# The input norm's weight row multiplied into x instead of into the weights, and head norms by Exp(-0.5 Ln a) with one Newton step

## The chip, the cores and the metric

The kernel runs on one core of a Trainium2 chip. A core has a matrix engine (TensorE, PE in the profile; its weight loads are listed apart as PEld) and three engines for everything else: VectorE (DVE), ScalarE (ACT) and GpSimd (POOL). Each takes its instructions in order from a queue of its own, and semaphores hold an instruction back until what it needs is there. SyncE (SP) issues the transfers between the core's memory (SBUF) and the chip's memory, in order too. TensorE writes to accumulator banks (PSUM). The metric is the device time of one execution in microseconds.

## The reference

One encoder block on x of 2048 rows by 1024, in float32. What matters here:

```python
def rms_norm(x, gain):
    y = x * lax.rsqrt(jnp.mean(x * x, axis=-1, keepdims=True) + EPS)
    return y * gain

h = rms_norm(x, norm_gain)          # norm_gain: one weight for each of the 1024 columns
proj = h @ w_in                     # q, k, v of mixers A and B, gates ga and gb, merge gates mg
qa = rms_norm(qa.reshape(bsz, S, 8, 64), q_norm_a) * scale     # head norms: 64 columns each
ka = rms_norm(ka.reshape(bsz, S, 2, 64), k_norm_a)             # and the same for qb, kb
ya = banded_attention(qa, ka, va, ...) * silu(ga)
yb = merged(dilated_group(qb[g], kb[g], vb[g], ...) for g in 3 groups) * silu(gb)
merged = sigmoid(mg0 + b0) * (ya @ w_branch_a) + sigmoid(mg1 + b1) * (yb @ w_branch_b)
out = x + merged @ w_out
```

The weight row of the first norm may be multiplied into the normed rows or into the rows of w_in: the product is the same. A head norm needs 1/sqrt(a) of one number a for each row and head.

## The kernel before

Every large product is made of float16 matmuls: each operand is split into a high part and a remainder ("hi" and "lo"; XH and XL of x, wh and wl of the weights), and three products are added. Each block of weights is first scaled by a power of two, found from its sum of squares. The program has three stages.

*The x stage (0 to 71 us).* Sixteen tiles of 128 rows of x are loaded. ScalarE squares each and sums along the row (`x_square`, L432). `x_stats` makes a of the sums of a group of tiles, and `x_newton` 1/sqrt(a); there are five groups, two of two tiles and three of four. VectorE multiplies the tile (`x_scale`, L446), TensorE transposes it in two halves into one of three PSUM buffers (L452), ScalarE copies a half out as XH (L455), VectorE writes XL (L459). When four tiles are done, TensorE starts on two columns of gates (`g_step`, matmuls of 128 by 512, L294), with further transposes in between. The gate weights graw are multiplied by the norm's weights on GpSimd (`g_gain`, L309), squared, scaled and split.

*The unit stage (71 to about 1305 us).* 14 units of eight pairs of row blocks each, 112 pairs: two units of kind A (16 pairs) and twelve of kind B, three for each of four head pairs. For a pair TensorE makes q, k and v (L620) into two PSUM banks (pj) that take turns. ScalarE copies q and k out (rw, L638) and the high part of v (vt, L650), VectorE the remainder of v (L656), which frees the bank. Then the head norm: ScalarE squares (L663), VectorE sums (L668, L669), a first guess of 1/sqrt(a) from the bits of a (`rs_guess`, L245), three Newton steps on GpSimd (`rs_newton`, L254 to L257), the product with it on VectorE (L680), the product with the head weights on GpSimd (L687), the split on ScalarE (L693), VectorE (L697) and GpSimd (L702), and a transposing transfer to kq. Attention follows some three pairs later: scores (L770), maxima (L785), exponentials (L793), a high part (p, L798) and a remainder (L802), a transposing transfer to pt, values (L819). In the third unit of each head pair (32 pairs in all, "merge pairs" below) the three groups of mixer B are also merged: small operations on VectorE (L964 to L977), products on GpSimd (L982), sums on VectorE (L988, L989).

Beside this, one unit ahead, the next unit's weights are loaded to wraw, multiplied by the norm's weights on GpSimd (`w_gain`, in four parts, L165), squared on ScalarE (L203), summed by a small matmul (L179) and split (L220, L226).

*The tail (from about 1305 us).* Merge gates, two more gates, the branch products and the output product, with sums of blocks that save one product in eight. Sums of blocks of x and their splits (L1171 to L1180) are VectorE's work. Here the weights' gain is on ScalarE (`gain` in `w_ready`, L1229), before the squares (L1235); L1304 and L1305 finish a gate.

The order on every engine is fixed when the program is built. Steps are put in a heap with due times, by tables such as `NORM` (times in a pair of `square, stats, newton, scale, gain, hi, lo, swap, turn`), and are written out as TensorE's instructions pass those times. No engine reorders anything at run time: a step that waits holds back all that stands behind it on its engine.

Of the kernel before, what the change touches and what calls it, by code (L numbers as in the profile page):

```python
# [31 lines left out]
D = 1024  # L32
# [8 lines left out]
SX = 2.0 ** 9  # L41
# [38 lines left out]
X_GP = (2.1, 5.694, 7.094, 7.694, 8.894, 10.194)  # L80
X_W = (14.0, 38.0, 48.0, 1.1, 4.8, 5.2, 6.3, 0.6, 50.255)
# [9 lines left out]
def block_kernel(tc, x, w_units, w_gate, w_mrg, w_out, w_bra, w_brf, gain, qkg, sink, bias_a, bias_b, b_merge, out):  # L91
# [34 lines left out]
    gn = cst.tile([128, NCH], F32, name="gn")  # L126
# [34 lines left out]

    def gains(raw, c0, n):

        v = raw[:, c0:c0 + 2, :n]
        G.tensor_tensor(v, v, gn[:, c0:c0 + 2].unsqueeze(2).to_broadcast([128, 2, n]), OP.mult)  # L165

    def w_gain(u, i):
        gains(wtiles[u][0], 2 * i, 384 if u < NU else 256)
# [73 lines left out]
    def rs_guess(a, n):  # L242

        y = sm.tile([128, 10], F32, name="rs_y")
        V.tensor_scalar(y[:, :n].bitcast(I32), a.bitcast(I32), -0.5, float(0x5F3759DF), OP.mult, OP.add)  # L245
        return y[:, :n]

    def rs_newton(a, yv, r, n, pool):
# [3 lines left out]
        for i in range(3):  # L252
            if pool:
                G.tensor_tensor(tv, yv, yv, OP.mult)  # L254
                G.tensor_tensor(tv, tv, a, OP.mult)
                G.tensor_scalar(tv, tv, -0.5, 1.5, OP.mult, OP.add)
                G.tensor_tensor(r if i == 2 else yv, tv, yv, OP.mult)  # L257
# [3 lines left out]
            V.scalar_tensor_tensor(r if i == 2 else yv, tv, 1.5, yv, OP.add, OP.mult)  # L261
# [45 lines left out]
    def g_gain(c, i):  # L307
        v = gw[c][0][:, 4 * i:4 * i + 4, :]
        G.tensor_tensor(v, v, gn[:, 4 * i:4 * i + 4].unsqueeze(2).to_broadcast([128, 4, 128]), OP.mult)  # L309

# [13 lines left out]
    def g_pow(c):  # L324
# [3 lines left out]
        V.tensor_scalar(ih[:], inv[:], 0.5 / SX, None, OP.mult)  # L328
# [115 lines left out]
    def x_scale(t):  # L444
        i = t - groups[t][0]
        V.tensor_scalar(xts[t][:], xts[t][:], xss[groups[t]][:, i:i + 1], None, OP.mult)  # L446
# [37 lines left out]
    at(.015, lambda: nc.sync.dma_start(out=gn[:], in_=gain))  # L484
# [28 lines left out]
    for c in range(2):  # L513
        b = X_G[c]
        chain([(b + X_GP[0] * i, g_gain, c, i) for i in range(2)]
              + [(b + d, f, c) for d, f in zip(X_GP[1:], (g_square, g_sum, g_pow, g_hi, g_lo))])
    at(X_W[0], w_load, 0)
    steps = [(X_W[2] + X_W[4], w_sum, 0), (X_W[2] + X_W[5], w_pow, 0)]
    for i in range(4):
        steps += [(X_W[1] + 1.9 * i, w_gain, 0, i), (X_W[2] + X_W[3] * i, w_square, 0, i),  # L520
# [24 lines left out]
    st.close()  # L545

# [1272 lines left out]
```

## Time and profile before

| | |
|---|---|
| median of three timed runs | 2131.88 us (2131.82 to 2137.91) |
| the profiled execution | 2139.63 us |
| its span, first to last instruction | 2136.9 us |
| mean granted TensorE clock | 0.959 |
| TensorE busy, share of the span | 91% |
| VectorE, ScalarE, GpSimd busy | 73%, 56%, 53% |
| busiest lines of TensorE | L620, three groups of 2816 matmuls |
| first wide matmul (L294) | 27.28 us |

A row of the profile that names a line and an operation gives out<-in by the program's names, the shape, a count, then busy time and mean nanoseconds of one, and after the second bar the engine's idle time just before such instructions and what ended it. In a timeline row stand start, length, engine, line, operation; idle time in brackets. The clock is the share of full speed that the chip granted TensorE. "PE pj L620 <- DVE vt L656" is TensorE waiting at line 620 until VectorE's line 656 was done.

### The profile page before, as it was taken

What the parts mean: (1) busy time and instruction counts of PE and PEld (TensorE: products, weight loads), DVE (VectorE), ACT (ScalarE), POOL (GpSimd) and SP (SyncE); (2) the same over time, 40 slices, a digit from 0 to 9 for tenths busy, and PEclk for the clock granted to TensorE, in tenths of its full rate; (3) what the DMA queues carried; (4) which work ended last, traced back from release to release, by engine and by line L of the source; (5) the groups of instructions that cost most, each with busy time, mean ns of one, the idle gap of its engine ahead of it and who ended that gap; (6) DMA issues with size and microseconds to landing.
All of it is one profiled execution on the core that took longest, in us unless ns stands there. A gap on an engine that the chain in (4) does not pass through costs nothing. (4 is left out here: it accounts for less than half of the span.)

```text
span 2136.9 us, 52081 instructions
## 1 busy us (share of the span) xinstructions
PE 1946.8 (91%) x19278; PEld 1474.4 (69%) x19278; DVE 1556.7 (73%) x3698; ACT 1186.3 (56%) x2743; POOL 1136.9 (53%) x2587
## 2 busy tenths in 40 slices
PE   6999999999899998999889999869999994799899
PEld 4568967888898988889888984324444454576565
DVE  6589869967887688767887677884674568756764
ACT  6477658866566665666566554554554644333331
POOL 4255555656666667656666665440110247656653
PEclk9999999999999999999999999979999996899999
DMA  5269878975776685866756665212442253353341
GB/s 224 77 115 195 156 145 148 195 161 120 149 139 130 144 156 118 172 130 132 155 107 141 118 125 137 74 50 89 134 137 100 98 168 106 118 157 100 114 129 65
DMA packets 595455, 279.35 MB, mean 131 GB/s; under 512 B 456832, under 2 KB 550144, under 8 KB 594176
## 3 DMA queue, kind: packets, MB, share of 16 engines
q1 hardware_dynamic: 595200, 276.03, 56.7%
q8 instruction: 150, 2.46, 0.5%
q14 instruction: 105, 0.86, 0.1%
HBM read 115.23 MB, written 50.59 MB: 78 GB/s over the span
## 5 line engine op out<-in xcount | busy, mean ns | idle before, releaser
L620 PE MATMUL pj<-wh,XH 128*128 128x128 f16 (+2 forms) x2816 | 718.9, 271 | 17.2 <-DVE vt L656 17.1
L620 PE MATMUL pj<-wl,XH 128*128 128x128 f16 (+2 forms) x2816 | 725.2, 271 | 0.0
L620 PE MATMUL pj<-wh,XL 128*128 128x128 f16 (+2 forms) x2816 | 722.3, 272 | 0.0
L620 PEld LDWEIGHTS <-XH 128*128 128x128 f16 x5632 | 580.9, 113 | 76.4 <-issue 19.6
L620 PEld LDWEIGHTS <-XL 128*128 128x128 f16 x2816 | 318.7, 113 | 25.3
L785 DVE CUSTOM_DVE_ANT_0 pr<-s,b,ubuf 128x256 f32<-128x256 f32 (+3 forms) x512 | 218.3, 463 | 8.6 <-PE s L770 4.7
L680 DVE TENSOR_TENSOR rw<-rw,qr 128x512 f32<-128x512 f32 (+1 forms) x112 | 118.4, 1057 | 139.7 <-POOL vt L649 79.0
L693 ACT ACTIVATE spl<-rw 128x512 f16<-128x512 f32 (+1 forms) x112 | 72.2, 645 | 233.7 <-POOL vt L649 200.4
L1618 PE MATMUL fps<-y,bigh 128*128 128x128 f16 x1792 | 164.1, 227 | 38.4 <-ACT t L1349 26.3
L802 DVE SCALAR_TENSOR_TENSOR p<-pr,p 128x512 f16<-128x512 f32 (+2 forms) x256 | 187.7, 733 | 7.6 <-ACT p L798 7.4
L1369 PEld LDWEIGHTS <-wh 128*128 128x128 f16 x896 | 89.4, 100 | 141.1 <-issue 41.5
L687 POOL TENSOR_TENSOR rw<-rw,g 128x128 f32<-128x128 f32 (+1 forms) x224 | 145.4, 668 | 73.2 <-DVE rw L680 67.8
L702 POOL COPY spl<-spl 128x256 f16<-128x256 f16 (+1 forms) x224 | 89.5, 429 | 177.5 <-DVE spl L697 175.0
L254 POOL TENSOR_TENSOR rs_t<-rs_y 128x8 f32<-128x8 f32 (+2 forms) x345 | 107.5, 312 | 137.5 <-DVE rs_y L245 99.2
L1618 PEld LDWEIGHTS <-bigh 128*128 128x128 f16 x1792 | 146.4, 102 | 45.2 <-issue 41.4
L770 PE MATMUL s<-kq 128*128 128x128 f16 (+1 forms) x1856 | 152.2, 220 | 26.3 <-DMA kq<-spl 23.0
L1692 PE MATMUL fps<-WOh,mf 128*128 128x512 f16 x448 | 146.9, 401 | 25.5 <-DVE xr L1699 25.5
L798 ACT ACTIVATE p<-pr 128x512 f16<-128x512 f32 (+2 forms) x256 | 159.3, 622 | 17.9 <-DMA pt<-p 10.4
L770 PEld LDWEIGHTS <-kq 128*128 128x128 f16 x2016 | 133.3, 99 | 44.4 <-issue 28.6
L1618 PE MATMUL fps<-y,bigl 128*128 128x128 f16 x896 | 161.6, 226 | 0.0
L1692 PEld LDWEIGHTS <-mf 128*128 128x128 f16 x672 | 67.7, 102 | 109.9 <-issue 42.6
L819 PE MATMUL pv<-vt,pt 128*128 128x65 f16 (+1 forms) x2784 | 134.1, 194 | 9.9 <-DMA pt<-p 8.9
(241 smaller groups left out, 4493.7 us busy)
## 6 DMA issues: line engine op xcount, KB each, us to landing
wraw<-in_w_units_dram SPq DMA_DIRECT2D x56, 384.0 KB, 4.6
g<-mgd SPq DMA_DIRECT2D x64, 256.0 KB, 5.9
mgd<-t SPq DMA_DIRECT2D x56, 256.0 KB, 2.1
wraw<-in_w_mrg_dram SPq DMA_DIRECT2D x44, 256.0 KB, 4.3
zd<-z SPq DMA_DIRECT2D x128, 66.0 KB, 1.8
zz<-zd SPq DMA_DIRECT2D x64, 132.0 KB, 2.8
xt<-in_x_dram SPq DMA_DIRECT2D x16, 512.0 KB, 9.0
ytd<-yo SPq DMA_DIRECT2D x32, 256.0 KB, 3.5
```

The source lines that it names most:

```text
L254: G.tensor_tensor(tv, yv, yv, OP.mult)
L620: out.append(lambda lhs=lhs, rhs=rhs, ch=ch, a=a, b=b, k=k: T.matmul(ps[:, a:b], lhsT=lhs[:, ch, :], rhs=rhs[:, ch, a:b], start=(k == 0), ...
L680: V.tensor_tensor(q, q, self.rr[:, :n].unsqueeze(2).to_broadcast([128, n, HD]), OP.mult)
L687: G.tensor_tensor(q[:, i, :un.nq, :], q[:, i, :un.nq, :], g, OP.mult)
L702: G.tensor_copy(sp[:, i, nh:, :, :], sp[:, i, nq:nh, ::-1, :])
L770: T.matmul(self.sv[j][:, o:o + k1 - k0], lhsT=q[:, h, :], rhs=kt[:, un.nq + kh + v * un.nk, k0:k1], start=(v == 0), stop=(v == 1))
L785: V.tensor_tensor_reduce(out=self.pv[:, j, self.p0:self.p0 + W], in0=self.sv[j], in1=un.bias[:, self.h0 + j, self.b0:self.b0 + W], scale=I ...
L798: A.activation(self.sp[:, :128 * n], self.pr, AF.Copy, scale=PSC)
L802: V.scalar_tensor_tensor(self.sp[:, 128 * n:], self.pr, PSC, self.sp[:, :128 * n], OP.mult, OP.subtract)
L819: T.matmul(self.po[:, j, :w], lhsT=p[:, n * j + s, :], rhs=un.v[key][:, vh, c0:c0 + w], start=(k == 0 and s == 0), stop=(k == 2 and s == n ...
L1618: out.append(lambda p=p, c=c, wl=wl, yl=yl, n=n: T.matmul(ps[:, 128 * p:128 * p + 128], lhsT=w[wl][:, i, c, p, :], rhs=y[:, yl, c, :], sta ...
L1692: out.append(lambda p=p, ml=ml, wl=wl, k=k: T.matmul(ps[:], lhsT=m[:, ml, p, :], rhs=WO[wl][:, i, p, :], start=(fresh and k == 0), stop=(k ...
```

## The change

The norm's weights are no longer multiplied into any weight block. All of `gains`, `w_gain`, `g_gain` and the tail's `gain` go. In their place the weight row is loaded once into all 128 partitions (gb, 128 by 1024), scaled to a power of two by its largest entry on VectorE, and `x_scale` multiplies by the row's 1/sqrt(a) and by gb in one instruction. The power of two is taken back in small factors (gp2, gi2) that other small scalings already had.

The first guess of 1/sqrt(a) is now Exp(-0.5 Ln a), two instructions on ScalarE, and one Newton step follows in place of three. This holds for the head norms and for x. At the end of the x stage a table set is named that has both Ln and Exp.

```diff
-    gn = cst.tile([128, NCH], F32, name="gn")
+    gp2, gi2 = [], []
...
-    def gains(raw, c0, n):
-        v = raw[:, c0:c0 + 2, :n]
-        G.tensor_tensor(v, v, gn[:, c0:c0 + 2].unsqueeze(2).to_broadcast([128, 2, n]), OP.mult)
-
-    def w_gain(u, i):
-        gains(wtiles[u][0], 2 * i, 384 if u < NU else 256)
...
     def rs_guess(a, n):
         y = sm.tile([128, 10], F32, name="rs_y")
-        V.tensor_scalar(y[:, :n].bitcast(I32), a.bitcast(I32), -0.5, float(0x5F3759DF), OP.mult, OP.add)
+        A.activation(y[:, :n], a, AF.Ln)
+        A.activation(y[:, :n], y[:, :n], AF.Exp, scale=-0.5)
         return y[:, :n]
...
-        for i in range(3):
-            if pool:
-                G.tensor_tensor(tv, yv, yv, OP.mult)
-                G.tensor_tensor(tv, tv, a, OP.mult)
-                G.tensor_scalar(tv, tv, -0.5, 1.5, OP.mult, OP.add)
-                G.tensor_tensor(r if i == 2 else yv, tv, yv, OP.mult)
-                continue
+        if pool:
+            G.tensor_tensor(tv, yv, yv, OP.mult)
+            G.tensor_tensor(tv, tv, a, OP.mult)
+            G.tensor_scalar(tv, tv, -0.5, 1.5, OP.mult, OP.add)
+            G.tensor_tensor(r, tv, yv, OP.mult)
+        else:
...
     def x_scale(t):
         i = t - groups[t][0]
-        V.tensor_scalar(xts[t][:], xts[t][:], xss[groups[t]][:, i:i + 1], None, OP.mult)
+        V.scalar_tensor_tensor(xts[t][:], xts[t][:], xss[groups[t]][:, i:i + 1], gb[:], OP.mult, OP.mult)
+
+    def gain_load():
+        nc.sync.dma_start(out=gb[:], in_=gain.broadcast_to([128, D]))
+
+    def gain_scale():
+        m = sm.tile([128, 1], F32, name="gm")
+        V.tensor_reduce(m[:], gb[:], AX.X, OP.max, apply_absolute_value=True)
+        s, i = pow2(m[:], "x")
+        V.tensor_scalar(gb[:], gb[:], s[:], 2.0 ** -14, OP.mult, OP.mult)
+        gp2.append(ucol())
+        gi2.append(ucol())
+        V.tensor_scalar(gp2[0][:], i[:], 2.0 ** 14, None, OP.mult)
+        V.tensor_scalar(gi2[0][:], s[:], 2.0 ** -14, None, OP.mult)
...
-    at(.015, lambda: nc.sync.dma_start(out=gn[:], in_=gain))
+    at(.025, gain_load)
+    at(X_GS, gain_scale)
...
     st.close()
+    A.preload_act_table_set("natural_log_exp_and_others")
...
-            V.tensor_scalar(self.wsc[:], inv[:], 2.0 ** 2 / SX, None, OP.mult)
+            V.tensor_scalar(self.wsc[:], inv[:], 2.0 ** 2 / SX, gp2[0][:], OP.mult, OP.mult)
...
-        def gain(c):
-            raw = wtiles[u][0]
-            A.activation(raw[:, c, :256], raw[:, c, :256], AF.Copy, scale=gn[:, c:c + 1])
```

With line numbers of its own, the changed program puts the new operations here. ScalarE in a merge pair, before (L663 is the square, L969 the merge's exponential, L793 the exponentials of scores, L798 their high part p, L843 a copy of values):

```order
L638 ACTIVATE rw<-pj 128x256
L650 ACTIVATE vt<-pj 128x2x64
L663 ACTIVATE spl<-rw 128x512
L969 ACTIVATE bm_e<-bm_e 128x12
L793 ACTIVATE pr<-pr,nmB 128x256 x2
L798 ACTIVATE p_14549<-pr 128x512
L843 ACTIVATE zz<-pv 128x2x65
```

And in the change, the same pair (L668 is the square, L238 Ln, L239 Exp, L803 p):

```order
L643 ACTIVATE rw<-pj 128x256
L655 ACTIVATE vt<-pj 128x2x64
L668 ACTIVATE spl<-rw 128x512
L974 ACTIVATE bm_e<-bm_e 128x12
L798 ACTIVATE pr<-pr,nmB 128x256 x2
L238 ACTIVATE rs_y<-qss 128x8
L239 ACTIVATE rs_y<-rs_y 128x8
L803 ACTIVATE p_14059<-pr 128x512
L848 ACTIVATE zz<-pv 128x2x65
```

Ln and Exp stand between the exponentials and p; Ln reads qss, which VectorE writes after it has summed ScalarE's squares. On VectorE of the change, around those sums (L673, L674; L977 to L982 are the merge, L807 the remainder of p, L790 the maxima, L685 the product with 1/sqrt(a)):

```order
L661 SCALAR_TENSOR_TENSOR vt<-pj,vt 128x2x64
L673 TENSOR_REDUCE qss<-spl 128x8
L674 TENSOR_SCALAR qss<-qss,ubuf 128x8
L977 TENSOR_TENSOR bm_d<-bm_e,zz 128x12
L978 TENSOR_TENSOR bm_s<-bm_d 128x4
L979 TENSOR_TENSOR bm_s<-bm_s,bm_d 128x4
L980 RECIPROCAL bm_s<-bm_s 128x4
L982 SCALAR_TENSOR_TENSOR bm_e<-bm_e,ubuf,bm_s 128x4 x3
L807 SCALAR_TENSOR_TENSOR p_14059<-pr,p_14059 128x512
```

The guess L245 is gone from behind the sums; the rest stands as before. In the pairs without a merge, L807 follows L674 at once. ScalarE at the start of the change's program (L421 is the square of a tile, L459 the copy to XH, L304 and L322 the gate weights):

```order
L421 ACT_TABLE_LOAD
L421 ACTIVATE jk,xss<-xt 128x1024 x2
L238 ACT_TABLE_LOAD
L238 ACTIVATE rs_y<-xss 128x2
L239 ACT_TABLE_LOAD
L239 ACTIVATE rs_y<-rs_y 128x2
L421 ACTIVATE jk,xss<-xt 128x1024 x3
L238 ACT_TABLE_LOAD
L238 ACTIVATE rs_y<-xss 128x2
L239 ACT_TABLE_LOAD
L239 ACTIVATE rs_y<-rs_y 128x2
L459 ACTIVATE XH<-s 128x4x128
```

Before, five squares stood here in a row behind one table load. In the change each of the five groups has a load ahead of Ln and one ahead of Exp, ten in all, and one more stands at the start of the unit stage and one ahead of the first Tanh of the tail.

More of the change, by code (lines that the diff above doesn't have):

```diff
@@ L40 @@
 VSC = 2.0 ** -16
-SX = 2.0 ** 9
+SX = 2.0 ** 8
 SE = S + 256
@@ L514, in block_kernel @@
         b = X_G[c]
-        chain([(b + X_GP[0] * i, g_gain, c, i) for i in range(2)]
-              + [(b + d, f, c) for d, f in zip(X_GP[1:], (g_square, g_sum, g_pow, g_hi, g_lo))])
+        chain([(b + d, f, c) for d, f in zip(X_GP[1:], (g_square, g_sum, g_pow, g_hi, g_lo))])
     at(X_W[0], w_load, 0)
@@ L519, in block_kernel @@
     for i in range(4):
-        steps += [(X_W[1] + 1.9 * i, w_gain, 0, i), (X_W[2] + X_W[3] * i, w_square, 0, i),
+        steps += [(X_W[2] + X_W[3] * i, w_square, 0, i),
                   (X_W[2] + X_W[6] + X_W[3] * i, w_hi, 0, i), (X_W[2] + X_W[6] + X_W[7] + X_W[3] * i, w_lo, 0, i)]
@@ L1045, in block_kernel @@
         for i in range(4):
-            steps += [(t + W_STEP[2] - W_STEP[6] + W_STEP[3] * i, w_gain, u + 1, i),
-                      (t + W_STEP[2] + W_STEP[3] * i, w_square, u + 1, i),
+            steps += [(t + W_STEP[2] + W_STEP[3] * i, w_square, u + 1, i),
                       (t + W_STEP[4] + W_STEP[3] * i, w_hi, u + 1, i),
@@ L1245, in power @@
             wtiles[u, "im"] = im = ucol()
[L1246 removed]
+            V.tensor_scalar(im[:], inv[:], 0.5 / SX, gp2[0][:], OP.mult, OP.mult)
         at(b, w_load, u)
         for i in range(4):
[L1250 to L1251 removed]
             at(b + 6.8 + 1.3 * i, square, i)
```

18 lines of the change are left out of this document (7 added, 11 removed).

## The prediction

> **What bounds the kernel now.** I read the page first, then busy time by stretch, TensorE's own waits, and the timeline of one long wait. The stretches (columns: time, length, busy time and instructions of PE, PEld, DVE, ACT, POOL, then granted clock, DMA share, GB/s):
>
> ```profile
> PE 1946.8 (91%) x19278; PEld 1474.4 (69%) x19278; DVE 1556.7 (73%) x3698; ACT 1186.3 (56%) x2743; POOL 1136.9 (53%) x2587
> ...
> 71.00:1305.00 1234.00, 1161.59 (x13740) 1024.76 (x13738) 961.93 (x2748) 780.54 (x1977) 768.73 (x2247) 0.98 0.73 143
> 550.00:600.00 50.00, 42.03 (x534) 40.12 (x532) 43.39 (x129) 27.22 (x71) 36.25 (x94) 0.90 0.75 143
> 1305.00:1435.00 130.00, 104.74 (x492) 47.33 (x493) 109.90 (x178) 65.21 (x127) 55.28 (x44) 0.92 0.22 72
> ```
>
> The unit stage (71 to 1305 us) is 58% of the span, and TensorE is busy in 1161.6 of its 1234 us: 72.4 us of waits are all that other engines can give back there. A second loss goes with them. The granted clock is 0.98 over the stage, 0.02 x 1234 = 25 us, and 0.90 in the stretch with the most waiting, so a microsecond waited costs about 25/72 = 0.34 more in clock. At most 97 us can be won here. TensorE's waits in the stage (total, times, longest):
>
> ```profile
> PE s L770 <- DMA kq<-spl: 23.0, 12, 4.5
> PE pj L620 <- DVE vt L656: 17.1, 10, 3.8
> PE pt L179 <- ACT wl L203: 10.7, 12, 1.4
> PE pv L819 <- DMA pt<-p: 8.9, 7, 2.7
> PE pt L883 <- DVE ya L989: 5.9, 4, 2.1
> ```
>
> What stands behind the second row is seen in the longest of its waits, near 581 us:
>
> ```profile
> 573.00 0.20 POOL L254 TENSOR_TENSOR rs_t<-rs_y 128x8 f32<-128x8 f32 x1 [0.54 <-DVE bm_d L972]
> 576.60 0.21 POOL L257 TENSOR_TENSOR qr<-rs_t,rs_y 128x8 f32<-128x8 f32 x1
> 576.76 2.21 POOL L982 TENSOR_TENSOR zz<-zz,bm_e 128x256 f32<-128x256 f32 x3
> 578.93 1.65 POOL L165 TENSOR_TENSOR wraw<-wraw,gn 128x768 f32<-128x768 f32 x1
> 580.61 0.84 ACT L203 ACTIVATE wl<-wraw 128x768 f16<-128x768 f32 x1 [3.68 <-POOL vw L649]
> 582.22 0.63 ACT L693 ACTIVATE spl<-rw 128x512 f16<-128x512 f32 x1 [0.67 <-POOL rw L687]
> 584.25 0.68 DVE L697 TENSOR_TENSOR spl<-rw,spl 128x512 f16<-128x512 f32 x1
> 584.85 0.27 DVE L656 SCALAR_TENSOR_TENSOR vt<-pj,vt 128x128 f16<-128x128 f32 x1
> ```
>
> Read down: GpSimd runs twelve Newton operations (573.00 to 576.81), the merge's products, and then a weight gain (L165). ScalarE's square L203 waits 3.68 us for that gain, so the split L693 behind it is late, VectorE's L697 too, and L656, in order behind L697, frees the PSUM bank only at 585.1. GpSimd's queue is what is late, not its share of 53%. The change shortens just this queue.
>
> **The head norms.** Their prices:
>
> ```profile
> L680 DVE TENSOR_TENSOR rw<-rw,qr 128x512 f32<-128x512 f32 x96 | 98.5, 1026 | 126.0 <-POOL vt L649 73.2 <-POOL qr L257 38.2 <-POOL vw L649 14.6
> L254 POOL TENSOR_TENSOR rs_t<-rs_y 128x8 f32<-128x8 f32 x288 | 87.2, 303 | 77.4 <-DVE rs_y L245 47.5 <-DVE bm_d L972 13.3 <-DVE wm L186 1.6
> L257 POOL TENSOR_TENSOR qr<-rs_t,rs_y 128x8 f32<-128x8 f32 x96 | 20.1, 209 | 8.0
> L969 ACT ACTIVATE bm_e<-bm_e 128x12 f32<-128x12 f32 x31 | 6.5, 211 | 1.4 <-DVE bm_e L966 1.4
> L165 POOL TENSOR_TENSOR wraw<-wraw,gn 128x768 f32<-128x768 f32 x52 | 78.7, 1514 | 0.0
> ```
>
> Twelve operations took 3.8 us; four of them take a third, 1.25. Saved: 2.55 us per pair. Added: Ln and Exp at 0.21 each (L969, an Exp of the same size; no trace shows Ln, which I take as equal), less VectorE's guess (0.17), with one more handoff of about 0.1: 0.35. So the scaled q and k come 2.2 us earlier. VectorE's wait at L680 is 126.0/96 = 1.31 us per pair of kind B, and less than the 2.2 saved: it should go. The new cost is a wait: Ln stands in ScalarE's queue behind the two exponentials and waits for VectorE's sums, and behind it queue the copy p (L798 before), the copies out of PSUM, and so VectorE's L802, which reads p. In the merge pairs VectorE has the merge's small operations in between, in kind A the two maxima; there the delay is covered, nearly or wholly. In the other B pairs it is not, but TensorE hardly waits in those. I set 4 us against it over the stage.
>
> **The weight gains.** L165 goes: 52 x 1.51 = 79 us of GpSimd, none of it directly on TensorE's path. The square L203 then waits for the load alone. Covered by nothing else, TensorE's 10.7 us on L203 go, but for about 1 us.
>
> **Sum of the unit stage.** The L656 row: two of 17.1 stay, so 15 back. The kq row: twelve waits, each shortened by at most 2.2 us, which for the long ones leaves a remainder that the weight loads in the same queue hold: 15 of 23.0 back. L203: 10. ya: 4 of 5.9. The pt row hangs on ScalarE's p, which comes no earlier: nothing. Together 44, with clock 0.34 x 44 = 15: 59. Less 4: **55 us won**; bounds 10 (only L203) and 97.
>
> On the clock the Trainium skill differs ("TensorE: Matmul & The Clock Gate", Part 1): it drops the clock after about 3.4 us of idleness. By that rule only the few longest waits would cost clock, some 7 us in place of 25; the row of the profile decides, since 0.98 is measured.
>
> **The first stage.** x times the gain now needs a broadcast row, its scale, and 10 more table loads on ScalarE, two for each of five groups of tiles.
>
> ```profile
> 0.74 1.28 ACT L432 ACT_TABLE_LOAD   x1 [0.74 <-PEq L1808]
> 7.62 1.06 ACT L432 ACTIVATE jk<-xt 128x1024 f16<-128x1024 f32 x1 [0.58 <-DMA xt<-in_x_dram]
> 8.90 1.06 ACT L432 ACTIVATE jk<-xt 128x1024 f16<-128x1024 f32 x1
> ...
> 9.24 0.75 DVE L446 TENSOR_SCALAR xt<-xt,xr 128x1024 f32<-128x1024 f32 x1
> 13.78 0.75 DVE L446 TENSOR_SCALAR xt<-xt,xr 128x1024 f32<-128x1024 f32 x1
> 24.75 1.50 DVE L446 TENSOR_SCALAR xt<-xt,xr 128x1024 f32<-128x1024 f32 x1 [1.72 <-POOL xr L257]
> 27.28 0.63 PE L294 MATMUL pj<-XH,gh 128*128 128x512 f16 x1
> L897 DVE TENSOR_REDUCE ymx<-yo 128x1 f32<-128x512 f32 x8 | 5.4, 676 | 0.0
> L455 ACT ACTIVATE XH<-s 128x512 f16<-128x512 f32 x32 | 18.8, 594 | 14.5 <-PE s L452 14.2
> L337 DVE SCALAR_TENSOR_TENSOR gl<-graw,ubuf,gh 128x1024 f16<-128x1024 f32 x2 | 2.6, 1282 | 0.0
> ```
>
> The gain row (512 KB in place of 4) takes a place among the x tiles, which come 1.28 us apart, and lands near 8.5. VectorE then reduces it (2 x 0.68), does seven small steps (0.2 each) and a scale (0.75): 12.0. Then the sums, Ln, a table load (1.28; the other one has run meanwhile), Exp, Newton: first x_scale at about 14.7, not 9.24. ScalarE has three squares (3 x 1.28) and then the second group's load, Ln, load, Exp (3.0): second x_scale at 21.4, not 13.78. Ten operations follow (five copies of 0.6, five squares or splits of 1.25: 9.2), the third group's 3.0 and GpSimd's Newton (1.5): the fifth x_scale comes at 34.5, not 24.75. The first matmul follows it by 2.5 us now and by 2.8 with the dearer x_scale (1.28 for 0.75, priced as L337): **10 us later**. The two later groups put 3 us each into a ScalarE queue that has little room; transposes have three buffers, so a part is absorbed: 3 more. Sum 13, bounds 8 (the row lands and is scaled while x waits) and 24 (each load at twice its row).
>
> That upper end has a rule behind it. The Trainium skill ("ScalarE: Activation LUTs", What ACT_TABLE_LOAD costs) gives 1.28 us for the load, as the row here does, and adds a drain of 1.38 for every switch of set; its table of sets speaks against this part, since one set holds both Ln and Exp, and this stage does not name it. The one load in this trace is followed by a wait for x, which hides any drain.
>
> **The tail.** The merge weights' gains on ScalarE (L1229) go:
>
> ```profile
> L1229 ACT ACTIVATE wraw<-wraw,gn 128x256 f32<-128x256 f32 x72 | 32.8, 494 | 1.9 <-DMA wraw<-in_w_mrg_dram 1.9
> 1347.66 0.66 DVE L1305 TENSOR_SCALAR t<-t 128x512 f32<-128x512 f32 x1 [1.75 <-ACT t L1304]
> 1386.70 0.81 DVE L1305 TENSOR_SCALAR t<-t 128x512 f32<-128x512 f32 x1 [3.54 <-ACT t L1304]
> ```
>
> From 1305 to 1435 us VectorE is the bound (109.9 of 130), and twice it waits for ScalarE just behind such gains. Eight gains make 8 x 0.41 = 3.3 us of the 3.54, and most of the 1.75: 5 us back, bounds 0 and 8. Later TensorE is full, and the gains are off the path. The one table load before Tanh falls into ScalarE's idle time. The factors folded into the small scales change no count.
>
> **Sum.** +13 - 55 - 5 = -47 us. The profiled execution took 2139.63 us (span 2136.9 and 2.7 around it), so 2092.6 for it. It lies 7.75 us above the median of 2131.88; from the median, **2085**.
>
> **The rivals.**
> (a) *A ring between ScalarE and VectorE*, slower. Ln waits for VectorE's sums, VectorE's L802 then waits for Ln, Exp and p (0.21 + 0.21 + 0.63 + 0.1 = 1.15 us per pair). In the merge stretch VectorE is busy 43.4 of 50 us and waits 1.31 x 4.5 pairs = 5.9 more (112 pairs in 1234 us are 11.0 each): 49.3 of 50. If L680's wait stays, the ring's 1.15 x 4.5 = 5.2 puts VectorE 4.5 us over in each such stretch, seven stretches for 32 pairs: 32 us; and 18 in the 16 pairs of kind A. With clock 67; only L203 (14 with clock) and the tail (5) come back: +13 + 67 - 19 = +61, 2193. It decides from 0.7 us of added wait per 50 us. Against it: the merge's own operations stand between sums and p. Chance 0.16.
> (b) *The waits move to the transfers*: kq and vt stay, because the queue's weight loads land when they do. Only L203 and the tail are won: +13 - 14 - 5 = -6, 2126. Chance 0.14, half of it on each side of the 0.3% that a measurement of this kernel can tell from no change (6.4 us).
> (c) *Dearer table switches*, each at two loads' time: the first matmul five loads later (6.4) and some 4 more behind, 2095. The rule above would do this. Chance 0.14.
> (d) *All waits of the unit stage go*: -97 + 13 - 5, 2043. Chance 0.08.
>
> My forecast has 0.48. Faster: 0.48 + 0.14 + 0.08 + 0.07 = 0.77; same 0.07; slower 0.16. The range runs from 2048, near (d), to 2130, past (b), and leaves out (a) and part of (d).
>
> **What would show it.** Right: the first wide matmul near 37 us; L680's wait under 0.3 us per pair; TensorE waiting under 35 us between the first pair and the tail; the L203 row gone. Wrong: VectorE waiting for p in the merge pairs (a), the kq row near 23 (b), a gap of over a microsecond behind each table load (c).

## The result, and the profile after

The changed kernel took **2054.82 us** (median of four runs, 2052.72 to 2057.84); the kernel before, on the same chip, 2131.85. The ratio is 0.9637, with a 95% interval of 0.9611 to 0.9663: faster by 77 us, where 47 was forecast. The forecast time of 2085 lay 30 us above the result, which lies in the lower part of the range.

First busy time by stretch, of before and then of after. The boundaries are the same places of the program: first and last matmul that makes q, k or v; first product of a sum of blocks (L1369, after: L1367); first branch product (L1618, after: L1616); the end. Columns as in the prediction: time, length, PE, PEld, DVE, ACT, POOL, clock, DMA share, GB/s.

```profile
81.14:1272.08 1190.94, 1123.94 (x13468) 1004.74 (x13467) 926.39 (x2642) 756.29 (x1923) 748.16 (x2207) 0.98 0.73 143
1272.08:1372.62 100.54, 94.38 (x572) 47.08 (x571) 82.59 (x189) 49.03 (x105) 50.89 (x68) 0.97 0.42 106
1372.62:1747.65 375.03, 344.65 (x1556) 154.75 (x1555) 242.63 (x426) 203.59 (x395) 88.64 (x80) 0.96 0.32 106
1747.65:2136.90 389.25, 321.62 (x3361) 230.19 (x3359) 248.81 (x312) 125.10 (x231) 223.20 (x176) 0.89 0.40 119
```

```profile
90.88:1200.25 1109.37, 1098.24 (x13468) 990.97 (x13467) 856.52 (x2542) 795.40 (x2147) 458.30 (x1268) 1.00 0.81 153
1200.25:1297.87 97.62, 92.97 (x573) 46.48 (x571) 77.52 (x180) 46.39 (x99) 42.34 (x50) 0.98 0.46 109
1297.87:1667.48 369.61, 344.62 (x1555) 154.77 (x1554) 245.93 (x426) 176.34 (x331) 88.97 (x80) 0.96 0.32 107
1667.48:2056.10 388.62, 323.94 (x3361) 232.22 (x3359) 247.96 (x312) 125.09 (x231) 223.03 (x176) 0.90 0.40 119
```

The first of them comes 9.7 us later (90.88 for 81.14). The unit stage between its first and last such matmul is 1109.4 us for 1190.9, **81.6 less**: TensorE waits 11.1 us in it where it waited 67.0, and the same 13468 matmuls take 25.7 less, at a clock of 1.00 for 0.98. The next two stretches give 2.9 and 5.4, the last 0.6. Together 9.7 - 81.6 - 8.9 = -80.8, the difference of the two spans. That is 4 us more than the 77 of the medians: the profiled execution of before took 2139.63 us, 7.8 over its median, that of after 2057.84, 3.0 over its own. The stretches are good to a few us, no better.

TensorE's waits that are left, from 71 to 1290 us, and four rows of VectorE (the maxima, the remainder of p, the product with 1/sqrt(a), the split):

```profile
PE pv L824 <- DMA pt<-p: 8.9, 8, 2.7
PE s L775 <- DMA kq<-spl: 4.9, 3, 4.5
PE pt L172 <- DVE yo L895: 0.9, 1, 0.9
PE s L775 <- DVE nmA L790: 0.8, 2, 0.5
```

```profile
L790 DVE CUSTOM_DVE_ANT_0 pr<-s,b,ubuf 128x256 f32<-128x256 f32 (+3 forms) x512 | 219.2, 465 | 70.2 <-PE s L775 66.9
L807 DVE SCALAR_TENSOR_TENSOR p<-pr,p 128x512 f16<-128x512 f32 (+2 forms) x256 | 194.9, 761 | 66.0 <-ACT p L803 62.0 <-DMA wraw<-in_w_units_dram 1.0
L685 DVE TENSOR_TENSOR rw<-rw,qr 128x512 f32<-128x512 f32 (+1 forms) x112 | 81.5, 727 | 0.0
L702 DVE TENSOR_TENSOR spl<-rw,spl 128x512 f16<-128x512 f32 (+1 forms) x112 | 79.2, 707 | 5.6 <-ACT spl L698 5.6
```

The waits for VectorE's remainder of v, for ScalarE's square and for ya are gone, and kq fell from 23.0 to 4.9. One wait of 4.5 us in that row lies behind the last matmul for q, k and v; inside the stage kq is 18.3 before and 0.4 after. L685 waits no more. VectorE now waits 66.9 us for TensorE's scores, where before it hardly waited for them:

```profile
L785 DVE CUSTOM_DVE_ANT_0 pr<-s,b,ubuf 128x256 f32<-128x256 f32 (+3 forms) x512 | 218.3, 463 | 8.6 <-PE s L770 4.7
L802 DVE SCALAR_TENSOR_TENSOR p<-pr,p 128x512 f16<-128x512 f32 (+2 forms) x256 | 187.7, 733 | 7.6 <-ACT p L798 7.4
```

So the order of who waits for whom has turned round. The page's chain that ended last says the same:

```profile
PE 74%; DVE 12%; DMA 5%; issue 3%; ACT 3%; POOL 2%; SPq 1%; DVEq 0%; POOLq 0%; ACTq 0%
```

TensorE's own work makes up three quarters of it. Two things stand out. VectorE waits 62.0 us for ScalarE's p (7.4 before), the new wait that the prediction named (in the pairs of kind A the trace has two maxima between L674 and L807, so there they do not follow at once). And L685 itself takes 727 ns, which it did not foresee; over all its forms it took before:

```profile
L680 DVE TENSOR_TENSOR rw<-rw,qr 128x512 f32<-128x512 f32 (+1 forms) x112 | 118.4, 1057 | 139.7 <-POOL vt L649 79.0 <-POOL qr L257 46.1 <-POOL vw L649 14.6
L697 DVE TENSOR_TENSOR spl<-rw,spl 128x512 f16<-128x512 f32 (+1 forms) x112 | 91.9, 821 | 45.4 <-ACT spl L693 45.4
```

The same instructions on tiles of the same shapes take 36.9 and 12.7 us less in all. The x stage, from the timeline of after (L444 reduces the weight row, L238 is Ln, L239 Exp, L435 the product):

```profile
8.95 1.22 DVE L444 TENSOR_REDUCE gm<-gb 128x1 f32<-128x1024 f32 x1 [8.95 <-DMA gb<-in_gain_dram]
11.96 0.20 ACT L238 ACTIVATE rs_y<-xss 128x2 f32<-128x2 f32 x1 [3.99 <-DVE xss L425]
12.18 1.28 ACT L239 ACT_TABLE_LOAD   x1
13.48 0.20 ACT L239 ACTIVATE rs_y<-rs_y 128x2 f32<-128x2 f32 x1
14.30 1.28 DVE L435 SCALAR_TENSOR_TENSOR xt<-xt,xr,gb 128x1024 f32<-128x1024 f32 x1
20.61 1.28 DVE L435 SCALAR_TENSOR_TENSOR xt<-xt,xr,gb 128x1024 f32<-128x1024 f32 x1
33.08 2.00 DVE L435 SCALAR_TENSOR_TENSOR xt<-xt,xr,gb 128x1024 f32<-128x1024 f32 x1
36.11 0.63 PE L287 MATMUL pj<-XH,gh 128*128 128x512 f16 x1
```

A load of 1.28 us stands between Ln and Exp with 0.02 us on either side. The first product of x came at 14.30 (forecast 14.7), the second at 20.61 (21.4), the fifth at 33.08 (34.5), the first wide matmul at 36.11 (37).

### The profile page after: what moved, and what is told of

Read it like the earlier page. It is cut to its first block, busy times and chain, and to the rows that moved or that the text cites. A ratio compares the mean times of both kernels' runs of the same rounds, so it can differ in the third digit from the quotient of the medians.

```text
span 2056.1 us, 50959 instructions
## 1 busy us (share of the span) xinstructions
PE 1923.4 (94%) x19278; PEld 1462.6 (71%) x19278; DVE 1488.5 (72%) x3578; ACT 1209.0 (59%) x2917; POOL 821.0 (40%) x1599
## 4 chain that ended last, share of the span: by engine, by line
PE 74%; DVE 12%; DMA 5%; issue 3%; ACT 3%; POOL 2%; SPq 1%; DVEq 0%; POOLq 0%; ACTq 0%
PE pj L625 40%; PE fps L1367 11%; PE fps L1616 6%; PE fps L1690 5%; PE s L775 4%; PE pv L824 4%; PE pj L287 3%; DMA pt<-p 2%; DVE mf L1663 2%; DVE t L1178 1%; DVE bigl L1184 1%; DVE t L1175 1%; PE fps L287 1%; DMA kq<-spl 1%; DVE wl L1275 1%
## 5 line engine op out<-in xcount | busy, mean ns | idle before, releaser
L625 PE MATMUL pj<-wl,XH 128*128 128x128 f16 (+2 forms) x2816 | 716.0, 268 | 0.0
L625 PE MATMUL pj<-wh,XL 128*128 128x128 f16 (+2 forms) x2816 | 712.3, 269 | 0.0
L625 PE MATMUL pj<-wh,XH 128*128 128x128 f16 (+2 forms) x2816 | 709.5, 268 | 0.0
L790 DVE CUSTOM_DVE_ANT_0 pr<-s,b,ubuf 128x256 f32<-128x256 f32 (+3 forms) x512 | 219.2, 465 | 70.2 <-PE s L775 66.9
L807 DVE SCALAR_TENSOR_TENSOR p<-pr,p 128x512 f16<-128x512 f32 (+2 forms) x256 | 194.9, 761 | 66.0 <-ACT p L803 62.0
L692 POOL TENSOR_TENSOR rw<-rw,g 128x128 f32<-128x128 f32 (+1 forms) x224 | 136.2, 628 | 210.9 <-DVE rw L685 191.4
L1616 PE MATMUL fps<-y,bigh 128*128 128x128 f16 x1792 | 166.3, 228 | 35.4 <-ACT t L1347 24.2
L1367 PEld LDWEIGHTS <-wh 128*128 128x128 f16 x896 | 89.3, 100 | 135.7 <-issue 36.0
L643 ACT ACTIVATE rw<-pj 128x256 f32<-128x256 f32 (+1 forms) x224 | 87.4, 390 | 167.1 <-PE pj L625 166.6
L1616 PEld LDWEIGHTS <-bigh 128*128 128x128 f16 x1792 | 147.7, 103 | 42.1 <-issue 38.1
L803 ACT ACTIVATE p<-pr 128x512 f16<-128x512 f32 (+2 forms) x256 | 157.7, 616 | 15.5 <-DMA pt<-p 10.9
L1616 PE MATMUL fps<-y,bigl 128*128 128x128 f16 x896 | 163.6, 228 | 0.0
L775 PEld LDWEIGHTS <-kq 128*128 128x128 f16 x2016 | 131.0, 98 | 22.2 <-issue 6.7
L1347 ACT ACTIVATE t<-fps 128x512 f32<-128x512 f32 x96 | 56.7, 591 | 144.4 <-PE fps L1616 111.2
L824 PEld LDWEIGHTS <-pt 128*128 128x128 f16 x3024 | 119.5, 97 | 24.6 <-DMA pt<-p 11.4
```

The lines of the kernel that those rows point to most:

```text
L625: out.append(lambda lhs=lhs, rhs=rhs, ch=ch, a=a, b=b, k=k: T.matmul(ps[:, a:b], lhsT=lhs[:, ch, :], rhs=rhs[:, ch, a:b], start=(k == 0), ...
L643: A.activation(self.rw[:, n * i:n * i + n], self.ps[i][:, :n], AF.Copy)
L692: G.tensor_tensor(q[:, i, :un.nq, :], q[:, i, :un.nq, :], g, OP.mult)
L775: T.matmul(self.sv[j][:, o:o + k1 - k0], lhsT=q[:, h, :], rhs=kt[:, un.nq + kh + v * un.nk, k0:k1], start=(v == 0), stop=(v == 1))
L790: V.tensor_tensor_reduce(out=self.pv[:, j, self.p0:self.p0 + W], in0=self.sv[j], in1=un.bias[:, self.h0 + j, self.b0:self.b0 + W], scale=I ...
L803: A.activation(self.sp[:, :128 * n], self.pr, AF.Copy, scale=PSC)
```

## The experiments

The theory at the outset, T: the unit stage won because the head norm's part in GpSimd's queue got shorter, the weight gains being the lesser half. Its rivals: the gains are the main thing (R1); a ring of ScalarE and VectorE costs time (R2). Times are medians. The runs stood on four chips; the kernel before, run beside each, took 2132.6 to 2134.9, and the ratios are to these. "Unit stage" is the stretch of the first row above and its waits are TensorE's idle time in it, both of one profiled execution of each kernel. A name with a + builds on x's old norm.

| kernel | us | ratio to before, 95% | first wide matmul | unit stage | waits in it |
|---|---|---|---|---|---|
| before | 2133.6 | | 27.3 | 1190.9 | 67.0 |
| the change, again | 2054.74 | 0.9616 to 0.9650 | 36.0 | 1105.7 | 9.2 |
| gain only | 2099.35 | 0.9818 to 0.9858 | 32.9 | 1155.9 | 42.7 |
| norms only | 2070.83 | 0.9679 to 0.9719 | 32.0 | 1122.7 | 20.0 |
| x's old norm | 2051.37 | 0.9596 to 0.9634 | 32.7 | 1110.1 | 11.5 |
| + heads' guess on VectorE, one step | 2049.06 | 0.9582 to 0.9620 | 32.3 | 1106.4 | 10.2 |
| + heads' three steps | 2118.75 | 0.9915 to 0.9958 | 32.3 | 1174.0 | 58.4 |
| + idle small operations | 2055.29 | 0.9608 to 0.9650 | 32.4 | 1113.1 | 15.7 |
| + weight row first | 2051.37 | 0.9593 to 0.9631 | 29.8 | 1111.6 | 13.1 |
| ... and heads' guess on VectorE, two steps | 2055.17 | 0.9621 to 0.9653 | 30.0 | 1115.4 | 16.5 |
| gain only + idle product | 2132.88 | 0.9986 to 1.0009 | 32.4 | 1188.7 | 69.8 |
| gain only + idle copy | 2132.67 | 0.9980 to 1.0007 | 32.3 | 1188.8 | 68.4 |
| gain only + idle constant | 2103.45 | 0.9851 to 0.9887 | 32.2 | 1156.1 | 48.1 |

### The two halves, each alone

Gain only: the change, with the norms as before.

```diff
-        A.activation(y[:, :n], a, AF.Ln)
-        A.activation(y[:, :n], y[:, :n], AF.Exp, scale=-0.5)
+        V.tensor_scalar(y[:, :n].bitcast(I32), a.bitcast(I32), -0.5, float(0x5F3759DF), OP.mult, OP.add)
...
+        for i in range(3):      # rs_newton
```

> Only the first half of the change: the norm's weights are multiplied into x; 1/sqrt(a) stays the guess from a's bits on VectorE with three Newton steps. Theory T (the unit stage won because GpSimd's part of a head norm, the eight Newton operations, got shorter; the weight gains are the lesser half): x stage 4 us later than before, L203's wait gone and a part of the wait for the remainder of v, tail -5: about 2106 us, TensorE's unit-stage waits still over 45 us and the kq row over 18. Rival R1 (the weight gains, 1.5 us each in GpSimd's queue, are the main thing): about 2070 us, kq row under 10.

Norms only: the kernel before, with the new norms.

```diff
+        V.tensor_scalar(xts[t][:], xts[t][:], xss[groups[t]][:, i:i + 1], None, OP.mult)
-        V.scalar_tensor_tensor(xts[t][:], xts[t][:], xss[groups[t]][:, i:i + 1], gb[:], OP.mult, OP.mult)
...
+            steps += [(t + W_STEP[2] - W_STEP[6] + W_STEP[3] * i, w_gain, u + 1, i),
```

> Only the second half: Ln, Exp and one Newton step for heads and x; the weights are multiplied as before, on GpSimd and in the tail on ScalarE. Theory T: x stage 5 to 8 us later than before (table loads alone), unit stage some 60 us shorter, with the wait on ScalarE's square of the weights (10.7 us before) still there; no gain in the tail: about 2079 us. Rival R1: kq row and the wait for v's remainder stay mostly, about 2115 us. If the two halves add up, the gains of this run and of the run with the gain alone sum to the 77 us of the whole.

Measured: 34 us won by the gain alone, 63 by the norms alone. T holds in the order of the two; both came out 7 to 8 us faster than it said, and the gain alone left 42.7 us of waits, a little under the 45 expected. They do not add up: 34 + 63 = 97 against 79 for both (2133.55 - 2054.74, on another chip). In the unit stage it is 35.0 + 68.2 against 81.6 to 85.2. TensorE's waits from 71 to 1290 us, of gain only and then of norms only:

```profile
PE s L774 <- DMA kq<-spl: 20.1, 9, 3.8
PE pj L624 <- DVE vt L660: 6.8, 4, 2.5
PE pt L172 <- ACT wl L196: 3.0, 2, 1.5
```

```profile
PE pt L179 <- ACT wl L203: 7.2, 4, 2.2
PE s L771 <- DMA kq<-spl: 5.3, 5, 2.9
PE pj L621 <- DVE vt L657: 1.0, 2, 0.5
```

The norms end most of the wait for kq and nearly all for v's remainder; the gain ends most of those for the square (10.7 to 3.0) and of those for v's remainder too (17.1 to 6.8), which is one place where the two overlap. In the stretch from 1372.6 the gain alone gives the tail's part (375.0 to 370.5 us), the norms alone none (375.0).

### x's table loads, and the wait behind Ln

x's old norm: the guess from the bits and three steps for x, Ln, Exp and one step for the heads.

```diff
-        xss[g] = [ss, rs_guess(ss, len(g))]
+        xss[g] = [ss, rs_guess(ss, len(g), False)]
...
-        rs_newton(ss, y, xss[g][:, :len(g)], len(g), len(g) > 2)
+        rs_newton(ss, y, xss[g][:, :len(g)], len(g), len(g) > 2, 3)
```

> As the change, but x's 1/sqrt(a) by the guess from the bits and three Newton steps, so that the five groups of x load no table; the head norms are as in the change. By the order of the x stage, two table loads of 1.28 us ahead of each of the first groups' products come off ScalarE's queue: first wide matmul at 30 to 32 us in place of 36.1, the unit stage unchanged, about 2049 us (-6 against the change). If the table loads were hidden by waits for x and for the weight row anyway: 2054 us.

And with the heads' guess on VectorE as well:

```diff
-    A.preload_act_table_set("natural_log_exp_and_others")
...
-            self.ss = ss[:, :n], rs_guess(ss[:, :n], n, True)
+            self.ss = ss[:, :n], rs_guess(ss[:, :n], n, False)
```

> As the run with x's old norm, but the head norms take their first guess from a's bits on VectorE and then one Newton step: no Ln, no Exp, no named table set. This alters the head norms' 1/sqrt(a), which is less exact by one step than three steps make it; the time is what is asked. It takes away the wait of ScalarE's queue for VectorE's sums and leaves the four GpSimd operations. Theory T (that wait costs little, as VectorE is not what sets the end): within 4 us of the run with x's old norm. Rival R2 (a ring of ScalarE and VectorE costs TensorE time): 15 us or more faster than it, and VectorE's wait for p (62 us in the change) nearly gone.

Measured: without x's loads the first wide matmul comes at 32.7 for 36.0 (30 to 32 expected), and 3.4 us are won in all (2054.74 to 2051.37, intervals that overlap). So the ten loads (13 in the change, 3 here) were on the path for 3.3 of their 12.8 us, and the weight row makes the rest of the delay: 32.9 us with the gain alone. Without Ln and Exp the heads win 3.7 us in the unit stage, where R2 asked for 15; it falls for this kernel, although most of VectorE's wait for p goes with them. First two rows of VectorE with Ln and Exp (x's old norm), then two without:

```profile
L811 DVE SCALAR_TENSOR_TENSOR p<-pr,p 128x512 f16<-128x512 f32 (+2 forms) x256 | 195.9, 765 | 66.6 <-ACT p L807 63.4
L794 DVE CUSTOM_DVE_ANT_0 pr<-s,b,ubuf 128x256 f32<-128x256 f32 (+3 forms) x512 | 219.0, 465 | 69.0 <-PE s L779 65.5
L810 DVE SCALAR_TENSOR_TENSOR p<-pr,p 128x512 f16<-128x512 f32 (+2 forms) x256 | 188.7, 737 | 21.0 <-ACT p L806 18.1
L793 DVE CUSTOM_DVE_ANT_0 pr<-s,b,ubuf 128x256 f32<-128x256 f32 (+3 forms) x512 | 219.1, 465 | 101.4 <-PE s L778 98.9
```

The wait for p falls from 63.4 to 18.1 us, and VectorE spends most of that time waiting for TensorE instead (65.5 to 98.9).

### Eight operations ahead of the product, or behind it

Three steps for the heads (on x's old norm):

```diff
-            rs_newton(*self.ss, self.rr[:, :n], n, True, 1)
+            rs_newton(*self.ss, self.rr[:, :n], n, True, 3)
```

> As the run with x's old norm, but the head norms make three Newton steps on GpSimd after Ln and Exp, not one: eight small operations more per pair, 2.5 us, ahead of the product with 1/sqrt(a). Theory T (the unit stage won through these eight): unit stage back near the 1156 us of the run with the gain alone, in all about 2097 us; TensorE waits for kq about 20 us. If the weight gains off GpSimd's queue were enough by themselves: under 2065 us.

One step, and eight operations that nobody reads, behind the product with the head weights:

```diff
                 G.tensor_tensor(q[:, i, :un.nq, :], q[:, i, :un.nq, :], g, OP.mult)
+            for i in range(8):
+                G.tensor_tensor(dm[:], dm[:], dm[:], OP.mult)
```

> As the run with x's old norm (one Newton step), and GpSimd does eight operations of 128 by 8 more in each pair, on a tile that nobody reads, behind the product with the head weights, where it has been waiting for the remainder from VectorE for some 2.2 us. GpSimd's queue is as full as with three Newton steps, but 1/sqrt(a) is as early as with one. Theory T1 (what counts is when 1/sqrt(a) is ready, the latency of the chain): within 8 us of the run with x's old norm. T2 (what counts is how full GpSimd's queue is): near the run with three steps, 30 us or more slower.

Measured: 67 us slower than one step, and 4 us slower (the second with intervals that overlap). Unit stages, of the first and of the second:

```profile
85.57:1259.57 1174.00, 1115.58 (x13468) 998.67 (x13467) 865.20 (x2531) 783.16 (x2146) 668.31 (x2150) 0.99 0.74 145
85.94:1199.03 1113.09, 1097.38 (x13468) 990.28 (x13467) 863.86 (x2542) 795.81 (x2147) 702.03 (x2152) 1.00 0.80 153
```

GpSimd runs as many instructions and is even busier in the second (702 us for 668). T1 holds: it is how late 1/sqrt(a) is, not how full the queue is. The expectation missed in the first: 67 us for 46. It is also 19 us slower than gain only, from which it differs, for the heads, in Ln and Exp alone. Two of its VectorE rows:

```profile
L689 DVE TENSOR_TENSOR rw<-rw,qr 128x512 f32<-128x512 f32 (+1 forms) x112 | 96.2, 859 | 132.9 <-POOL vt L658 84.1 <-POOL qr L254 37.1 <-POOL vw L658 11.8
L811 DVE SCALAR_TENSOR_TENSOR p<-pr,p 128x512 f16<-128x512 f32 (+2 forms) x256 | 188.5, 736 | 52.0 <-ACT p L807 50.7 <-DMA wraw<-in_w_units_dram 1.0 <-ACT spl L702 0.2
```

VectorE waits both for 1/sqrt(a) (132.9 us, 96.3 with the gain alone) and for p (50.7, 9.9 with the gain alone). That fits the ring of rival (a) under the condition that it named, that the wait for 1/sqrt(a) stays, and the price is 18 us in the unit stage (1174.0 against 1155.9). It is not shown that the ring is all of it: with Ln and Exp the first Newton operation also starts 0.60 us after VectorE's sums, and 0.30 with the guess from the bits (means of the 112 pairs in the two traces), so 1/sqrt(a) comes 0.3 us later in each pair. No run parts the two.

### What the gains cost: a queue, or a lock

Gain only, and GpSimd does a product on an idle tile where each gain stood; then a copy; then a constant written:

```diff
+    def w_idle(u, i):
+        v = dm[0][:, :, :384 if u < NU else 256]      # 128 x 768 float32
+        G.tensor_tensor(v, v, v, OP.mult)
...
+        G.tensor_copy(v, v)                           # the second: 128 x 1536 float16
...
+        G.memset(v, 1.0)                              # the third: the same tile
...
+            steps += [(t + W_STEP[2] - W_STEP[6] + W_STEP[3] * i, w_idle, u + 1, i),
```

> As the run with the gain alone (three Newton steps, 2099 us), and GpSimd does a product of 128 by 768 on a tile that nobody reads at the times at which the weights' gains stood before. The queue is as full as before, but ScalarE's square of the weights waits for the load only. Unit stage before 1191 us, with the gain alone 1156. If the gains cost their 35 us by holding back the Newton steps queued behind them: 1180 us or more, 2123 in all. If by the square that waits for them and holds ScalarE's queue: under 1165, 2108 in all.

> As the run with the idle product at the times of the gains (2133 us), and the idle operation is a copy of 128 by 1536 float16, one input in place of two, of about the same length. In the run with the idle product VectorE's product with 1/sqrt(a) took 1967 ns in the 17 pairs in which it stood beside that product, and 715 ns in those with nothing beside it. Theory C (two-input products of GpSimd and VectorE hold each other up, and the gains cost their 35 us so): VectorE's product stays near 715 ns beside the copy, unit stage near the 1156 us of the run with the gain alone, 2100 to 2108 in all. Theory Q (GpSimd's queue alone, whatever runs in it): again 1180 us or more, 2123 or more in all.

> As the run with the idle copy, and the idle operation writes a constant to the same tile and reads nothing: one of these took 1.38 us, the copy 1.46. Beside the copy, VectorE's product with 1/sqrt(a) ended 0.55 to 0.68 us after the copy's end, its own length after it, so it had been held for the whole copy. The Trainium skill (SBUF - State Buffer, the section on ports) states a lock: an operation of VectorE with two inputs in SBUF and one of GpSimd that reads SBUF exclude each other, and one that only writes does not. By the lock: the product takes about 715 ns beside this one too, unit stage 1156 to 1165 us, 2100 to 2108 in all. By GpSimd's queue alone, which is as full as with the copy: 1180 us or more, 2123 or more in all.

Measured: 2132.88, 2132.67, 2103.45. The first settles that no data dependence is needed for the 35 us. The second let theory C fall as it was put: the copy, with one input, cost as much. But in the timeline the copy does to VectorE what the gain did, and the constant does not. First a pair of rows of before, then of the copy, then of the constant:

```profile
95.15 1.47 POOL L165 TENSOR_TENSOR wraw<-wraw,gn 128x768 f32<-128x768 f32 x1
95.19 2.11 DVE L680 TENSOR_TENSOR rw<-rw,qr 128x640 f32<-128x640 f32 x1 [1.34 <-POOL vt L649]
```

```profile
297.73 1.46 POOL L171 COPY dm<-dm 128x1536 f16<-128x1536 f16 x1
297.78 2.09 DVE L693 TENSOR_TENSOR rw<-rw,qr 128x640 f32<-128x640 f32 x1 [1.88 <-POOL vt L662]
```

```profile
111.20 1.38 POOL L171 MEMSET dm<- 128x1536 f16 x1
111.30 0.82 DVE L693 TENSOR_TENSOR rw<-rw,qr 128x640 f32<-128x640 f32 x1 [3.29 <-POOL qr L259]
```

Beside the gain and beside the copy, VectorE's product ends 0.68 us after GpSimd's operation has ended, and takes 2.1 us; beside a write of a constant it takes 0.82 and ends before it. So it goes in all the pairs: the 20 products of before that overlap a gain end 0.54 to 0.68 us after the gain does, and so do the 18 beside a copy; the 16 beside a constant take 0.68 to 0.83 us and end before it. The Trainium skill says this ("SBUF — State Buffer", Who interferes with whom): VectorE's second input and GpSimd share one interface, held by one instruction until it ends, so an operation of VectorE with two inputs in SBUF and one of GpSimd that reads SBUF shut each other out. These rows agree. The queue theory falls: GpSimd is about as busy with the constant as with the copy (729 and 746 us), and 33 us of the unit stage go, down to the 1156 us of the gain alone. Unit stages of the copy and of the constant:

```profile
85.45:1274.23 1188.78, 1120.34 (x13468) 1000.64 (x13467) 925.37 (x2643) 753.22 (x1923) 745.53 (x2208) 0.99 0.74 143
86.48:1242.60 1156.12, 1107.97 (x13468) 994.61 (x13467) 887.00 (x2642) 756.63 (x1923) 729.19 (x2207) 0.99 0.76 147
```

### Better versions

The weight row loaded ahead of x, on x's old norm:

```diff
+    at(-.01, gain_load)
     for t in range(XT_BUFS):
         at(.01 * t, x_load, t)
-    at(.025, gain_load)
```

> As the run with x's old norm, and the weight row is loaded ahead of the first tile of x, not behind the third: its scaling on VectorE (9.3 to 12.1 us there) then lies in the wait for x. The row takes 1.25 us of the transfers: first product of x at 10.8 us in place of 14.3, first wide matmul at 29 to 30 in place of 32.7, in all 3 us less, about 2048. If the later tiles of x set the first wide matmul, and not the first product: no change, 2051.

The same with the heads' guess from the bits and two steps (1/sqrt(a) is less exact than with three):

```diff
-            rs_newton(*self.ss, self.rr[:, :n], n, True, 1)
+            rs_newton(*self.ss, self.rr[:, :n], n, True, 2)
```

> As the run with the weight row first, but the head norms take the guess from a's bits on VectorE and two Newton steps, without Ln, Exp or the named table set: four GpSimd operations more than the change, 1.25 us, and ScalarE's two fewer. If TensorE's waits grow with each operation that is added (67 us for eight behind Ln and Exp, 49 for eight behind the guess): some 25 us more, 2073. If there is slack of over 0.9 us in the chain after the first step, as the 2 us between Ln and Exp and the guess with one step suggest: under 2056.

> The change once more, on the same chip as the other two: 2052 to 2058 us.

The first matmul comes 2.9 us earlier as expected (29.8), but the time is that without it, 2051.37; a difference of this size is not told apart from run to run. Two steps from the bits cost 4 us against one step behind Ln and Exp (1115.4 and 1111.6 in the unit stage), far from the 25 that a cost per operation would make. With the guess from the bits the unit stage is 1106.4 us with one step, 1115.4 with two and 1155.9 with three: the first four operations more cost 9 us, the next four 40. The chain has slack, and the third step uses it up: VectorE's wait at the product with 1/sqrt(a) is 0.0, 7.3 and 96.3 us in the three. The fastest versions (2049 to 2051) lie 3 to 6 us under the change, about 0.2%, with intervals that overlap its own; in the one of 2049 us, one step from the bits, 1/sqrt(a) is less exact than in the change.

## Why the prediction came out as it did

*In all, forecast -47, measured -77.* The time lies inside the stated range, but the range is 82 us wide, and 2054.8 is nearer to rival (d), 2043, than to the forecast of 2085. The x stage and the tail came within 4 us of their terms; the unit stage was mis-sized.

*The unit stage, forecast -55, measured -81.6: the term that was mis-sized.* The first half of the mechanism was right: the shorter chain on GpSimd is the larger half, and L680's wait went as worked out (0.0 for the 0.3 allowed). The step that failed was the count of what would be left. Waits: 44 forecast, 55.9 measured (67.0 to 11.1). Inside the stage kq gave 17.9 and not 15, the L656 row 17.1 and not 15, the L203 row 9.4 for the 10, ya all of its 5.9 and not 4, and three small rows of before, which the forecast did not count, gave 5.4 of their 7.1:

```profile
PE pt L179 <- DVE yo L890: 3.1, 1, 3.1
PE s L770 <- DVE nmA L785: 3.0, 5, 0.7
PE pv L819 <- ACT pr L793: 1.0, 1, 1.0
```

Clock: 15 forecast from 0.34 us for each us waited; the same matmuls took 25.7 less. The 4 us set against the wait at Ln are near what the runs show: one step behind Ln and Exp was 3.7 us slower in the stage than one step behind VectorE's guess, though the medians (2051.37 and 2049.06) have intervals that overlap. pt was forecast at nothing, and kept its 8.9.

*A hidden part: what the weight gains cost.* The prediction gave the weight gains no direct effect on VectorE: "none of it directly on TensorE's path", and only the square's wait as theirs: 10 us and 3.4 of clock. Its own row, L680 with a mean of 1026 ns, held the hint: left alone it takes little more than 0.7, as after's 727 ns show. In the run with the gain alone the two rows of VectorE are:

```profile
L684 DVE TENSOR_TENSOR rw<-rw,qr 128x512 f32<-128x512 f32 (+1 forms) x112 | 95.7, 855 | 96.3 <-POOL vt L653 60.2 <-POOL qr L250 25.7 <-POOL vw L653 10.3
L701 DVE TENSOR_TENSOR spl<-rw,spl 128x512 f16<-128x512 f32 (+1 forms) x112 | 79.2, 708 | 26.4 <-ACT spl L697 26.2
```

That is 22.7 us off the first (118.4 before) and 12.7 off the second (91.9). The merge's small operations and sums fell too: in the stage VectorE was busy for 926.4 us before and for 886.0 with the gain alone, 40.4 less for as many instructions (2642), and the stage is 35.0 shorter. The gains were worth that, not the 14 of rival (b), which counted L203 and its clock. The prediction priced them by ScalarE's square, which waits for the gain as GpSimd's queue lets it through. This part of the mechanism was wrong: the idle product costs as much with no square waiting for it, and the idle constant, about as long in the queue, at most 4 us (2103.45 against 2099.35). By halves the forecast was 42 for the norms (34 of waits and 12 of clock, less 4) and 13 for the gains; alone they gave 68.2 and 35.0. That the time came out inside the range is owed in part to the range's width, and to the two halves giving less together than apart.

*The clock.* By the Trainium skill's rule ("TensorE: Matmul & The Clock Gate", Part 1) the prediction saw some 7 us to come back, and by the profile's row 25. The clock records of the traces decide it: stretches in which the chip granted half of the clock cost the stage 22.2 us before and 1.7 after, so 20.5 came back; the other 5 of the 25.7 are not explained. The rule as the prediction put it, 3.4 us of idleness, does not hold here: in before half clock came eleven times, for 3.4 or 6.8 us each, and ten of these followed single waits of 2.3 to 4.5 us, seven of them under 3.4. Nor is the loss a price for each us waited: the gain alone lost 13.7 us in seven such stretches with 42.7 us of waits, the idle constant 6.8 in three with 48.1. It goes by the number of long waits, and not even by that strictly, since waits of 3.0 and 3.8 us in these two had no half clock behind them.

*The x stage, forecast +13, measured +9.7.* The first wide matmul came 8.8 us later for the 10, the later groups' loads 0.9 for the 3 (the rest of the 9.7); that the transposes' buffers absorbed them, as forecast for a part, is not shown. Alone, the norms made it 4.7 later and the gain 5.6.

*The tail, forecast -5, measured -8.9* over three stretches. The gain alone shows 4.5 of it to be the gains on ScalarE. The other two stretches, 2.9 and 0.6, are not told apart from what differs from run to run.

*The rivals.* (a) was half there: the wait of VectorE for p came (62.0 us), the sign by which the text would have called it, but VectorE no longer set the end, and taking Ln and Exp away won only the 3.7 us above. In the run with three steps, where the condition in its text is met (the wait for 1/sqrt(a) stays), Ln and Exp cost 18 us and not 67, the ring and the later 1/sqrt(a) together. (b) fell: kq went from 23.0 to 4.9, so the weight loads in SyncE's queue were not what held most of it. (c) fell, with a first wide matmul at 36.1 and not near 43: the Trainium skill's drain of 1.38 us for each switch ("ScalarE: Activation LUTs", What ACT_TABLE_LOAD costs) does not show in the rows above, where Exp starts 0.02 us after the load, and the load 0.02 after Ln. Ten loads fewer gave 3.4 us. (d), 2043, is what the unit stage came nearest to (-97 in its text); most of the waits that kept it from there are pt's 8.9.

## What to carry to other kernels

Where in-order engines pass one piece of work round, count the time from hand to hand and not the share of an engine: eight small operations ahead of a handoff cost 67 us here, the same eight behind it 4, on an engine busy half of the time. When one instruction's mean is well above that of its fastest instances, look at what runs beside it before looking at what it waits for; and when a shortened chain ends a wait, ask which engine waits next, since a new wait on an engine that no longer sets the end costs little (here 62 us of it some 4).

## What the runs showed of the hardware

GpSimd and VectorE shut each other out where GpSimd reads SBUF and VectorE reads two inputs there: the product of 128 by 640 took 2.1 us beside a copy of 1.46, and 0.82 beside a constant of 1.38. It goes both ways: with the norms alone two products started 0.3 and 0.5 us ahead of a gain, and there the gain took 1.9 us for its usual 1.47. Two inputs are not needed in every form, as the x stage of before shows. The product of x at 24.75 us in the prediction, with one tile and a number for each row, took 1.50 us where others took 0.75, and started beside this gain:

```profile
24.67 1.04 POOL L309 TENSOR_TENSOR graw<-graw,gn 128x512 f32<-128x512 f32 x1
```

It ended 0.54 us after the gain. In the change the fifth product of x (33.08, 2.00 us for 1.28) stood beside copies on GpSimd.

In the run with the norms alone, where the gains are still there, the product with 1/sqrt(a) is hardly held:

```profile
L681 DVE TENSOR_TENSOR rw<-rw,qr 128x512 f32<-128x512 f32 (+1 forms) x112 | 86.5, 773 | 0.0
```

It waits no more for GpSimd (0.0), and so no longer starts in the instant in which GpSimd goes on to the gain. Other operations are held still: VectorE is busy for 881.7 us in that unit stage and for 856.5 in the change's, with 2542 instructions in both, 25 us of the 40 between before and the gain alone. These 25 cost 13 us of the stage (1122.7 against 1109.4), where the 40 cost 35 beside three steps. That VectorE then has time to spare, so that being held costs less, would be why the two halves win less together than apart; it is read from the rows, and was not tested by itself.
